# Gates and the first half's u by seven products per 2x2 block, in a hybrid attention and gMLP block on one Trainium2 core

## Chip, cores and metric

The kernel runs on one core of one Trainium2 chip. The metric is device time in microseconds: the median of the runs shown. Everything is float32; matmuls take float32 operands split into a high and a low part in a rounded 32-bit form (fp32r), so that one exact product costs three matmuls: high x high, high x low and low x high.

## The reference, cut to what matters

```python
h = rmsnorm(x, norm_pre_mix)                      # x: 2048 tokens x 1024
proj = h @ w_in                                   # 1024 -> 5376 columns
q, k, v = rope(proj[Q]), rope(proj[K]), proj[V]   # 12 heads of 64, in 3 groups of dilation 1, 4, 16
u, z = gelu(proj[U]), gelu(proj[Z])               # 512 columns each
gate_a, gate_b = sigmoid(proj[GA]), sigmoid(proj[GB])   # 1024 columns each
y_attn = dilated_window_attention(q, k, v)        # three groups, combined by a softmax over log-denominators
y_gmlp = u * (w_spatial @ layernorm(z) + b_spatial)     # per chunk of 128 tokens, causal
merged = gate_a * (y_attn @ w_branch_attn) + gate_b * (y_gmlp @ w_branch_gmlp)
x = x + rmsnorm(merged @ w_out, norm_post_mix)
a = relu(rmsnorm(x, norm_pre_mlp) @ w_mlp_in)
return x + rmsnorm((a * a) @ w_mlp_out, norm_post_mlp)
```

## The kernel before, in words

Tokens are taken in four chunks `c` of 512; chunks 0 and 1 are the first half (`half` 0), 2 and 3 the second (`half` 1). The columns of `w_in` lie in 21 slabs of 256: 0 to 5 are q and k, 6 to 8 v, 9 and 10 u, 11 and 12 z, 13 to 20 the gates. A slab of 256 columns and a half of two chunks make a 2x2 block of outputs (two column groups `m` of 128, two chunks), and the depth of 1024 splits into two parts of four K-tiles of 128.

**Projections (0 to 422 us).** Per half: normalized tokens are transposed into `hT[c]` (high and low, 4 MB a chunk) by `prenorm_cols`; `v_block` makes v, then `qk_pair` makes q and k with the rope, one slab and chunk at a time, while `load_w` brings the next slab and splits it (high on GpSimd, low on VectorE). `keep_cols` writes a raw copy of chunks 0 and 1 to `hT_d` in DRAM, since only two chunks stay on chip.

**The filler.** `filler` is a generator over `queue`: u and z of the second half, the eight gate slabs for the second half, the same eight for the first half, then u and z of the first half. One step is one K-tile: three matmuls (`mm3`). Every slab of a half is 2 x 2 x 8 = 32 steps, 96 matmuls. `reload_h` brings chunks 0 and 1 back from `hT_d` and splits them again on GpSimd, when the first half's turn comes. Each output of 128 x 512 is evicted by ScalarE and written to `gate_d` or `u_d`; the sigmoid is applied later, in the merge.

**Attention (from about 515 us).** 48 units `(g, c, j)`: three groups, four blocks of 512 queries, four heads. TensorE's order is written out by hand: the scores of unit n, one filler step, the transposes `pT` of the exponentials of unit n-1, six filler steps, its product `pv` with v, two filler steps, its transposes back `po`. Keys and queries are loaded two units ahead (`attn_load`). Scores, transposes, `pv` and `po` use four PSUM banks (`aux`), the filler four others (`mm`). The four engines beside TensorE get their order from the scheduler of the framework, with the priorities of the program text; `behind()` ties a group of instructions behind what has been issued.

**Combination (about 990 to 1058 us).** For each chunk `combine` loads the three groups' outputs (`A`, two places), scales and adds them on VectorE (some adds on GpSimd), transposes the sum on TensorE and writes `ya_d`. Between the chunks stand 33, 21, 20 and 24 filler steps. Then z of the first half, the gMLP's `sz_out`, the merge with the gates, `w_out`, and the MLP, which already makes its products by seven instead of eight.

The DMA queue of SyncE (`sp.dma_start`) takes most loads and stores, in order of issue; ScalarE (`act`) and GpSimd (`pool`) can issue too. The page calls it SPq, ACTq and POOLq.

## Time and profile before

| | |
|---|---|
| median of 3 runs | 2687.41 us (2686.49 to 2688.89) |
| the profiled execution | 2693.87 us |
| its span, first to last instruction | 2692.1 us |
| mean granted TensorE clock | 0.998 |
| matmuls of the gates | 514 to 1013 us |
| u of the first half | 1014 to 1060 us |
| z of the first half | 1060 to 1104 us |
| moved by DMA | 431.77 MB, 160 GB/s over the span |

An engine is named PE (TensorE), PEld (its weight loads), DVE (VectorE), ACT (ScalarE), POOL (GpSimd) or SP (SyncE). Busy is the time in which the engine ran an instruction. In a group's row, what stands behind the second bar is the time for which the engine sat idle just ahead of those instructions, and what ended it. The DMA share is the mean busy share of the 16 DMA engines.

### The profile page before, as it was taken

To read this page: it belongs to the slowest core of one execution; us is meant where nothing else is said; L and a number is where in the kernel's file an instruction comes from. 1 tells how busy PE (TensorE), PEld (TensorE's weight loads), DVE (VectorE), ACT (ScalarE), POOL (GpSimd) and SP (SyncE) were. 2 spreads that over 40 slices of the span, in tenths; PEclk is the share of its full clock that TensorE was granted. 3 is DMA by queue.
4 is the path that set the end of the run, shared out by engine and by line. 5 is a ranking of instruction groups with operands and counts; after the bars stand their busy time and mean duration, and the time that the engine had idled before them with its cause. 6 is when DMAs were issued, how large, how long until landed. Compare 5 with 4: busy or idle time off the path is not lost. (4 is left out here: it accounts for less than half of the span.)

```text
span 2692.1 us, 34831 instructions
## 1 busy us (share of the span) xinstructions
PE 2660.2 (99%) x12674; PEld 2222.2 (83%) x12674; DVE 1591.5 (59%) x2677; ACT 1052.7 (39%) x2149; POOL 979.1 (36%) x843
## 2 busy tenths in 40 slices
PE   9999999999999999999999999999999999999998
PEld 7888888888888888888778888888888888888886
DVE  5665463334444435665567765555437888888866
ACT  5212111144444422344445555555545333233334
POOL 0352253200050004310233464323314776676644
PEclk9999999999999999999999999999999999999999
DMA  7445446366587846644576465554343212222235
GB/s 270 169 141 184 152 141 212 99 192 200 172 253 202 219 150 202 211 158 140 189 241 242 141 204 168 181 179 129 108 145 120 87 56 87 93 86 87 87 111 210
DMA packets 299198, 431.77 MB, mean 160 GB/s; under 512 B 52818, under 2 KB 166226, under 8 KB 299027
## 3 DMA queue, kind: packets, MB, share of 16 engines
q1 hardware_dynamic: 226000, 367.34, 43.1%
q10 hardware_dynamic: 64178, 32.06, 4.0%
q0 software_dynamic: 8848, 30.15, 2.9%
q8 instruction: 100, 1.64, 0.3%
q14 instruction: 72, 0.58, 0.1%
HBM read 286.67 MB, written 142.80 MB: 160 GB/s over the span
## 5 line engine op out<-in xcount | busy, mean ns | idle before, releaser
L1637 PE MATMUL ya<-T_spots,s 128*128 128x512 f32 x1176 | 289.2, 389 | 0.7 <-ACT T_spots L70 0.5
L1637 PEld LDWEIGHTS ya<-T_spots,s 128*128 128x128 f32 x1176 | 220.5, 188 | 47.3 <-ACT T_spots L70 0.9
L70 ACT ACTIVATE s<-sraw 128x768 fp32r<-128x768 f32 (+1 forms) x184 | 127.2, 696 | 330.3 <-POOL sraw L1438 156.0
L78 DVE TENSOR_TENSOR s<-sraw,s 128x512 fp32r<-128x512 f32 x172 | 184.3, 1096 | 8.5 <-ACT s L70 8.5
L1112 PE MATMUL aa<-B,A 128*128 128x512 f32 x768 | 182.0, 389 | 0.7 <-DVE A L85 0.7
L1112 PEld LDWEIGHTS aa<-B,A 128*128 128x128 f32 x768 | 143.9, 188 | 30.9 <-DVE A L85 1.1
L1637 PE MATMUL yc<-T_spots,s 128*128 128x512 f32 x624 | 159.6, 389 | 0.0
L72 POOL TENSOR_SCALAR w_g<-w_g_r 128x1024 fp32r<-128x1024 f32 x32 | 34.1, 1081 | 344.8 <-PE g L97 258.1
L1083 POOL TENSOR_TENSOR s<-w1r 128x512 f32<-128x512 f32 x32 | 42.3, 1323 | 308.8 <-DVE S L78 269.2
L95 PE MATMUL x<-hT_a,wq 128*128 128x512 f32 x384 | 149.7, 390 | 0.0
L96 PE MATMUL x<-hT_a,wq 128*128 128x512 f32 x384 | 149.4, 389 | 0.0
L97 PE MATMUL x<-hT_a,wq 128*128 128x512 f32 x384 | 149.4, 389 | 0.0
L709 DVE TENSOR_REDUCE o<-po 128x256 f32<-128x512 f32 x48 | 33.1, 691 | 184.5 <-PE po L708 184.5
L1637 PEld LDWEIGHTS yc<-T_spots,s 128*128 128x128 f32 x624 | 117.1, 188 | 24.3
L70 ACT ACTIVATE hl<-r 128x512 fp32r<-128x512 f32 x48 | 30.4, 633 | 238.1 <-POOL r L307 89.0
L78 POOL TENSOR_TENSOR T_spots<-w2r,T_spots 128x512 fp32r<-128x512 f32 x70 | 104.5, 1520 | 7.3 <-ACT T_spots L70 7.3
L95 PE MATMUL g<-hT_b,w_g 128*128 128x512 f32 x256 | 104.7, 409 | 0.0
L95 PE MATMUL g<-hT_a,w_g 128*128 128x512 f32 x256 | 104.2, 407 | 0.0
L95 PE MATMUL o<-wo,mg 128*128 128x512 f32 x256 | 101.2, 395 | 3.1 <-ACT mg L70 3.1
L70 ACT ACTIVATE S<-w1r 128x512 fp32r<-128x512 f32 x96 | 60.1, 629 | 104.8 <-PE ac L1112 62.9
L97 PE MATMUL o<-wo,mg 128*128 128x512 f32 x256 | 100.7, 394 | 0.0
L1437 POOL TENSOR_TENSOR sraw<-sraw 128x256 f32<-128x256 f32 x56 | 41.8, 746 | 161.7 <-DVE s L78 158.7
(391 smaller groups left out, 7218.9 us busy)
## 6 DMA issues: line engine op xcount, KB each, us to landing
w1r<-in_w_mlp_in_dram SPq DMA_DIRECT2D x64, 512.0 KB, 3.6
sraw<-sd SPq DMA_DIRECT2D x128, 256.0 KB, 3.3
qk<-hl SPq DMA_DIRECT2D x24, 1024.0 KB, 5.1
qq<-qk SPq DMA_DIRECT2D x96, 256.0 KB, 4.9
w_g_r<-in_w_in_dram SPq DMA_DIRECT2D x32, 512.0 KB, 4.9
gated<-gt SPq DMA_DIRECT2D x64, 256.0 KB, 3.4
w2r<-in_w_mlp_out_dram SPq DMA_DIRECT2D x16, 1024.0 KB, 6.3
sd<-u ACTq DMA_DIRECT2D x63, 256.0 KB, 3.5
```

Source lines behind the costliest of these rows:

```text
L70: act.activation(hi, src, AF.Copy)
L72: pool.tensor_scalar(hi, src, 1.0, 1.0, op0=OP.mult, op1=OP.mult)
L78: (pool if lo_eng == "pool" else dve).tensor_sub(lo, src, f32(hi))
L95: pe.matmul(ps, lh, rh, start=start, stop=False)
L96: pe.matmul(ps, lh, rl, start=False, stop=False)
L97: pe.matmul(ps, ll, rh, start=False, stop=stop)
L709: dve.tensor_reduce(ot[:, :, j * 64:(j + 1) * 64], po.rearrange("p (b h e) -> p b e h", b=4, h=2), axis=AX.X, op=OP.add)
L1083: pool.tensor_add(s1, a21, a22)
L1112: pe.matmul(p, w[:, l, k, :], h[:, r, k, :], start=i in (1, 6, 5) and not k and not n, stop=k == 3 and n == 2, skip_group_check=True)
L1437: pool.tensor_add(a22, a21, a22)
L1637: pe.matmul(p, s[:, l], w[r], start=i in (1, 2, 5) and not m and not o, stop=m == 1 and o == 2, skip_group_check=True)
```

## The change

Every 2x2 block of the gates in both halves, and of u in the first half, is made by seven products (Winograd's form of Strassen's) in place of eight. A product is one combination of four weight blocks (128 columns by four K-tiles, a "piece") with one combination of four token blocks (512 tokens by four K-tiles, an "operand"). The seven products are made in four phases, `(1, 2), (6, 7), (5, 3), (4,)`; in a phase one token operand serves all eight pairs of columns (second half) or ten (first half, with u) in turn, and the partial results wait in SBUF (`xs`, `zs`, `vs`), added up by VectorE.

- The sums of token blocks (`pre_t`) and of weight blocks (`pre_s`) are made ahead by VectorE and written to DRAM (`tg_d`, `sg_d`, `s1g_d`) by GpSimd's queue: 28 makers while q and k are projected, 8 more during u of the second half. High and low of chunks 0, 1 and half of 3 go to `hb_d`, raw copies of all four chunks to `hT_d`.
- In the gates each product loads its piece four products ahead, 128 x 512 values in runs of 512 B (2 KB for operand 5), and splits it three products ahead, high and low on GpSimd (high on ScalarE at the two ends). Operands are loaded a phase ahead; those from `tg_d` are split by ScalarE and GpSimd.
- `reload_h` loads high and low ready-made and splits nothing.
- From unit 4 on five filler steps stand between `pT` and `pv` instead of six. The combination gets four places for `A`, all loaded and worked on ahead, with 40, 12, 12 and 11 filler steps. `kp` has three places instead of four.

The diff, cut to its core:

```diff
--- before.py
+++ after.py
...
-    hT_d = dtile([2, P, KT, 512], "hTd")
+    hT_d = dtile([4, P, KT, 512], "hTd")
+    hb_d = dtile([4, P, 2, KT, 512], "hbd")
+    tg_d = dtile([2, P, 4, 4, 512], "tgd")
+    sg_d = dtile([10, P, 2, 4, 256], "sgd")
+    s1g_d = dtile([10, P, 4, P], "s1gd")
...
+        if i == 3:
+            ks = slice(4 if c == 3 else 0, KT)
+            if c != 2:
+                for o in range(2):
+                    sp.dma_start(hb_d[c][:, o, ks], f32(h)[:, o, ks])
...
-            if c < 2:
+            if c == 2 and i % 2:
+                raw = rp.tile([P, 4, P], F32, name=f"hr_{c}{i}{k}", tag="vt", bufs=2)
+            else:
                 raw = xp.tile([P, 4, P], F32, name=f"hr_{c}{i}{k}", tag="hr", bufs=3)
-                act.activation(raw, p3, AF.Copy)
-                sp.dma_start(hT_d[c, :, k:k + 4, i * P:(i + 1) * P], raw)
+            act.activation(raw, p3, AF.Copy)
+            (sp if c < 2 else act).dma_start(hT_d[c, :, k:k + 4, i * P:(i + 1) * P], raw)
...
         for k in range(0, KT, 2):
-            split_in(hT[c][:, :, k:k + 2], hT_d[c, :, k:k + 2, :], None, "pool", "pool")
+            for o in range(2):
+                sp.dma_start(f32(hT[c])[:, o, k:k + 2], hb_d[c][:, o, k:k + 2])
+    def w_at(n):
+        return 13 + n if n < 8 else 1 + n
...
+        def pre_t(half, k, j):
+            w = pre.tile([P, 5 if half else 4, 256], F32, name=f"pt{half}{k}{j}", tag="pre")
+            tsl = slice(j * 256, (j + 1) * 256)
+            for c in range(2):
+                sp.dma_start(w[:, 2 * c:2 * c + 2], hT_d[2 * half + c][:, k::4, tsl])
+            yield
+            b11, b21, b12, b22 = (w[:, n] for n in range(4))
+            dve.tensor_sub(b11, b12, b11)
+            dve.tensor_sub(b12, b22, b12)
+            dve.tensor_sub(b22, b22, b11)
+            dve.tensor_sub(b21, b21, b22)
+            yield
+            pool.dma_start(tg_d[half][:, :, k, tsl], w[:, :4])
+            yield
+        def pre_s(n, k):
+            w = pre.tile([P, 5, 256], F32, name=f"ps{n}{k}", tag="pre")
+            both = w[:, :4].rearrange("p (h k) c -> p h (k c)", h=2)
+            sp.dma_start(both, a["w_in"][w_at(n)].rearrange("p (h k) c -> p h k c", h=2)[:, :, k:k + 2].rearrange("p h k c -> p h (k c)"))
+            yield
+            a11, a21, a12, a22 = (w[:, 2 * kk:2 * kk + 2, m * P:(m + 1) * P] for kk in range(2) for m in range(2))
+            s1 = w[:, 4].rearrange("p (k c) -> p k c", k=2)
+            dve.tensor_add(s1, a21, a22)
+            dve.tensor_sub(a21, a11, a21)
+            dve.tensor_sub(a11, s1, a11)
+            dve.tensor_sub(a12, a12, a11)
+            yield
+            pool.dma_start(sg_d[n][:, :, k:k + 2].rearrange("p h k c -> p h (k c)"), both)
+            pool.dma_start(s1g_d[n][:, k:k + 2], s1)
+            yield
...
+        halves = [[(h_, k, j) for k in range(4) for j in range(2)] for h_ in range(2)]
+        makers = [lambda n=n, k=k: pre_s(n, k) for n in range(10) for k in (0, 2)]
+        makers[12:12] = [lambda z=z: pre_t(*z) for z in halves[1]]
+        flow = []
+        def pre_step():
+            with behind():
+                if makers:
+                    flow.append(makers.pop(0)())
+                for g in reversed(flow):
+                    next(g)
+                if len(flow) == 3 or not makers:
+                    flow.pop(0)
...
                 qk_pair(rp, w, g, which, 2 * half, ropes[2 * half])
+                pre_step()
...
+                pre_step()
+                if half and n % 3 == 2:
+                    pre_step()
+        while flow:
+            pre_step()
+        makers += [lambda z=z: pre_t(*z) for z in halves[0]]
...
-            (dve if c < 2 and g % 2 else pool).tensor_mul(t, t, ut)
+            (dve if c == 3 or c < 2 and g % 2 else pool).tensor_mul(t, t, ut)
...
     queue = [(9, "u", 0, 1), (10, "u", 1, 1), (11, "z", 0, 1), (12, "z", 1, 1)]
-    queue += [(13 + n, "g", n, 1) for n in range(8)] + [(13 + n, "g", n, 0) for n in range(8)]
-    queue += [(9, "u", 0, 0), (10, "u", 1, 0), (11, "z", 0, 0), (12, "z", 1, 0)]
+    queue += [(13, "g", 0, 1)]
+    queue += [(11, "z", 0, 0), (12, "z", 1, 0)]
...
+    PHASES = ((1, 2), (6, 7), (5, 3), (4,))
+    def lagged(ops, pairs):
+        first = [(n, (ops[0], n)) for n in range(pairs)]
+        return [z for _, z in sorted(first + [(n + 1.5, (i, n)) for n in range(pairs) for i in ops[1:]])]
+    PAIRS = {1: 8, 0: 10}
+    PIECES, SPLITS = 4, 3
+    seq = [(half, i, n) for half in (1, 0) for ops in PHASES for i, n in lagged(ops, PAIRS[half])]
+    LAST = len(seq) - PAIRS[0]
+    g_ = dict(raw={}, w={}, b={})
+    def piece(t):
+        if t >= len(seq):
+            return
+        half, i, n = seq[t]
+        raws = g_["raws"]
+        r = raws[t % 4] if t < 8 else raws[4 + (t - LAST - 4) % 5] if t >= LAST + 4 else raws[(t - 8) % 5]
+        if i < 3:
+            src = w_src(w_at(n), i - 1)[:, :, :P]
+        elif i == 5:
+            src = s1g_d[n]
+        else:
+            kk, m = {6: (0, 0), 7: (0, 1), 3: (1, 0), 4: (1, 1)}[i]
+            src = sg_d[n][:, kk, :, m * P:(m + 1) * P]
+        sp.dma_start(r.rearrange("p (k c) -> p k c", k=4), src)
+        g_["raw"][t] = r
+    def split_piece(t):
+        if t >= len(seq):
+            return
+        if t == 4:
+            g_["spots"].append(wp.tile([P, 4, 2, 4, P], F32R, name="spots1", tag="w", bufs=3))
+        at_ = t % 4 if t >= LAST else t % 8
+        w = g_["spots"][at_ // 4][:, at_ % 4]
+        split(w[:, 0], w[:, 1], g_["raw"].pop(t).rearrange("p (k c) -> p k c", k=4),
+              "act" if t < 12 or t > LAST - 10 else "pool", "pool")
+        g_["w"][t] = w
+    def operand(half, i, slot):
+        c = 2 * half
+        g_["b"][half, i] = slot
+        if i in (1, 2, 3):
+            src = hb_d[c + (i == 3)][:, :, (0, 4, 4)[i - 1]:][:, :, :4]
+            for o in range(2):
+                sp.dma_start(f32(slot)[:, o], src[:, o])
+            return []
+        src = tg_d[half][:, (5, 4, 7, 6).index(i)]
+        for k in range(0, 4, 2):
+            sp.dma_start(f32(slot)[:, 1, k:k + 2], src[:, k:k + 2])
+        return [(slot, k) for k in (0, 2)]
...
+    def gates_ahead():
+        g_["spots"] = [wp.tile([P, 4, 2, 4, P], F32R, name="spots0", tag="w", bufs=3)]
+        g_["raws"] = [w[:, m] for w in (wp.tile([P, 2, 512], F32, name=f"gr{n}", tag="raw", bufs=2) for n in range(2))
+                      for m in range(2)]
+        for t in range(PIECES):
+            piece(t)
+        for t in range(SPLITS):
+            split_piece(t)
+    def gates():
+        bank, todo, out_ = {}, [], []
+        slots = [None, hp.tile([P, 2, 2, 4, 512], F32R, name="opB", tag="hT", bufs=2)]
+        zs = wp.tile([P, 8, 512], F32, name="gz", tag="w", bufs=3)
+        zs = [zs[:, n] for n in range(8)]
+        xs = [st.tile([P, 512], F32, name=f"gx{n}", tag="ev", bufs=3) for n in range(3)]
+        g_["b"].update({(1, 1): hT[2][:, :, :4], (1, 2): hT[2][:, :, 4:]})
+        phases = [(half, ops) for half in (1, 0) for ops in PHASES]
+        starts, t = {}, 0
+        for n, (half, ops) in enumerate(phases):
+            starts[t] = n
+            t += PAIRS[half] * len(ops)
+        for t, (half, i, n) in enumerate(seq):
+            if t in starts:
+                ph, t0 = starts[t], t
+                if ph + 1 < len(phases):
+                    s = (ph + 1) % 2
+                    if not slots[s]:
+                        slots[s] = hp.tile([P, 2, 2, 4, 512], F32R, name="opA", tag="hT", bufs=2)
+                    for j, i2 in enumerate(phases[ph + 1][1]):
+                        todo += operand(phases[ph + 1][0], i2, slots[s][:, j])
+                else:
+                    reload_h(0)
+            elif todo and (t - t0) % 3 == 1 and t > t0 + 1:
+                w, k = todo.pop(0)
+                with behind():
+                    split(w[:, 0, k:k + 2], w[:, 1, k:k + 2], f32(w)[:, 1, k:k + 2], "act", "pool")
+            if t == LAST + 2:
+                want(5)
+            piece(t + PIECES)
+            split_piece(t + SPLITS)
+            if i in (1, 6, 5, 4):
+                bank[n] = psum_mm(f"g{half}{i}{n}")
+            p, w, h = bank[n], g_["w"].pop(t), g_["b"][half, i]
+            for k in range(4):
+                for m, (l, r) in enumerate(((0, 0), (0, 1), (1, 0))):
+                    pe.matmul(p, w[:, l, k], h[:, r, k], start=i in (1, 6, 5, 4) and not k and not m,
+                              stop=k == 3 and m == 2, skip_group_check=True)
+                if (t, k) == (3, 2) and late:
+                    sz_out(*late.pop(0))
+                yield
+            if t == 3:
+                a = [ga.tile([P, 512], F32, name=f"ga{n_}", tag=f"ga{n_}", bufs=1) for n_ in range(12)]
+                xs += a[:7]
+                zs += a[7:9]
+                vs = a[9:11]
+                g_["raws"] += a[11:] + vs + zs[8:]
+            x, z, fn = xs[n], zs[n], AF.Copy if n < 8 else AF.Gelu_apprx_tanh
+            while out_:
+                sp.dma_start(*out_.pop())
+            if i == 1:
+                act.activation(x, p, AF.Copy)
+            elif i == 2:
+                act.activation(z, p, fn)
+                o = z, 0, 0
+            elif i == 6:
+                dve.tensor_add(z, x, p)
+            elif i == 7:
+                dve.tensor_add(x, x, p)
+            elif i == 5:
+                v = vs[n % 2]
+                dve.tensor_add(v, x, p)
+                o = v, 1, 1
+            elif i == 3:
+                dve.tensor_add(z, z, p)
+                o = z, 0, 1
+            else:
+                dve.tensor_add(x, x, p)
+                o = x, 1, 0
+            if n > 7 and i in (5, 3, 4):
+                act.activation(o[0], o[0], fn)
+            if i in (2, 5, 3, 4):
+                c, dst = 2 * half + o[2], gate_d if n < 8 else u_d
+                out_.append((dst[n % 8 * 2 + o[1], :, c * 512:(c + 1) * 512], o[0]))
+        sp.dma_start(*out_.pop())
+        yield
...
+            if kind == "g":
+                yield from gates()
+                continue
...
+                if not half:
+                    reload_h(1)
                 for ci in range(2):
-                    yield from z_chunk(zps[half], w, half * 2 + ci)
+                    for k, _ in enumerate(z_chunk(zps[half], w, half * 2 + ci)):
+                        yield
+                        if half and k == 10 and (makers or flow):
+                            pre_step()
+                    if half and not ci:
+                        gates_ahead()
...
+            for c in (2, 3):
                 for m in range(2):
-                    p = psum_mm(f"{kind}_{n}{m}{c}")
-                    for sn, _ in enumerate(steps_T(w, m, c, p)):
-                        if kind == "g" and m == 1 and sn == 6 and late:
-                            sz_out(*late.pop(0))
-                        yield
-                    t = st.tile([P, 512], F32, name=f"{kind}t_{n}{m}{c}", tag="ev", bufs=3)
-                    act.activation(t, p, AF.Copy if kind == "g" else AF.Gelu_apprx_tanh)
-                    dst = gate_d if kind == "g" else u_d
-                    sp.dma_start(dst[n * 2 + m, :, c * 512:(c + 1) * 512], t)
+                    p = psum_mm(f"u_{n}{m}{c}")
+                    yield from steps_T(w, m, c, p)
+                    t = st.tile([P, 512], F32, name=f"ut_{n}{m}{c}", tag="ev", bufs=3)
+                    act.activation(t, p, AF.Gelu_apprx_tanh)
+                    sp.dma_start(u_d[n * 2 + m, :, c * 512:(c + 1) * 512], t)
+                    pre_step()
...
-        kp = at1.tile([P, 5 * P], F32R, name=f"kp_{nm}", tag="akp", bufs=4)
+        kp = at1.tile([P, 5 * P], F32R, name=f"kp_{nm}", tag="akp", bufs=3)
...
-        A = cb.tile([P, 4, 3, 264], F32, name=f"A_{c}", tag="cA", bufs=2)
+        A = cb.tile([P, 4, 3, 264], F32, name=f"A_{c}", tag="cA", bufs=4)
...
-            steps(6 if n > 1 else 9)
+            steps((6 if n < 4 else 5) if n > 1 else 9)
...
     cs = [combine(c) for c in (2, 3, 0, 1)]
     for n in range(2):
+        for z in cs:
+            next(z)
+    for n in range(4):
+        steps((40, 12, 12, 11)[n])
         next(cs[n])
-        next(cs[n])
-    for n in range(4):
-        steps((33, 21, 20, 24)[n])
-        next(cs[n])
-        if n < 2:
-            next(cs[n + 2])
-            next(cs[n + 2])
     ec.close()
+    ega.close()
```

More of the change, by code (lines that the diff above doesn't have):

```diff
@@ L521, in want @@
             else:
[L522 removed]
+                loaded[q] = load_w(wi, f"w_{kind}{n}{half}")
+    PHASES = ((1, 2), (6, 7), (5, 3), (4,))
[5 more added lines that the diff above has]
+    seq = [(half, i, n) for half in (1, 0) for ops in PHASES for i, n in lagged(ops, PAIRS[half])]
```

14 lines of the change are left out of this document (7 added, 7 removed).

## The prediction

> **What bounds the kernel now.** I read the page first, then the busy times by stretch, then the groups of instructions, then one attention unit on the timeline, then the DMA queues.
>
> ```profile
> span 2692.1 us, 34831 instructions
> PE 2660.2 (99%) x12674; PEld 2222.2 (83%) x12674; DVE 1591.5 (59%) x2677; ACT 1052.7 (39%) x2149; POOL 979.1 (36%) x843
> ```
>
> The profiled execution took 2693.87 us, 1.8 us more than this span and 6.46 us more than the median of the runs (2687.41); I sum against 2693.87 and take off 6.46 at the end. TensorE is the bound. The next answer is the busy time by stretch (stretch; its length; busy us and count of PE, PEld, DVE, ACT, POOL; clock; DMA share; GB/s):
>
> ```profile
> 25.00:50.00 25.00, 24.47 (x148) 21.45 (x147) 12.94 (x32) 12.34 (x30) 0.00 (x0) 1.00 0.91 302
> 300.00:400.00 100.00, 100.00 (x443) 82.81 (x442) 57.47 (x65) 11.39 (x18) 47.31 (x28) 1.00 0.45 150
> 400.00:500.00 100.00, 100.00 (x441) 82.44 (x440) 35.34 (x49) 15.84 (x24) 23.61 (x15) 1.00 0.46 155
> 514.00:1014.00 500.00, 498.06 (x2799) 428.01 (x2798) 210.58 (x675) 202.99 (x615) 76.32 (x61) 1.00 0.68 198
> 775.00:800.00 25.00, 25.00 (x149) 21.73 (x148) 12.65 (x35) 10.16 (x31) 22.78 (x14) 1.00 0.89 292
> 800.00:825.00 25.00, 25.00 (x145) 21.68 (x145) 10.49 (x29) 11.70 (x37) 2.08 (x2) 1.00 0.76 203
> 825.00:975.00 150.00, 149.27 (x834) 127.42 (x833) 59.36 (x228) 62.42 (x202) 10.30 (x10) 1.00 0.69 187
> 1014.00:1060.00 46.00, 46.00 (x216) 38.34 (x215) 26.15 (x64) 14.63 (x21) 20.93 (x10) 1.00 0.70 220
> ```
>
> From 514 to 1060 us lie the 48 attention units with the gates as filler, then the combination over the first half's u. TensorE idles 2 us of the first 500; DVE, ACT and POOL are 42%, 41% and 15% busy. So a matmul taken out here shortens the kernel by its own pitch, unless a new wait appears. The pitch is not the 389 ns of a single matmul, since they overlap: 400 to 500 us is unbroken 128x512 matmuls, 441 in 100 us, 0.2268 us each.
>
> **What is removed.** The groups by line and shape (count; busy, mean ns; idle before):
>
> ```profile
> L95 PE MATMUL g<-hT_b,w_g 128*128 128x512 f32 x256 | 104.7, 409 | 0.0
> L549 ACT ACTIVATE gt<-g 128x512 f32<-128x512 f32 x64 | 37.9, 593 | 62.6 <-PE g L97 47.0 <-issue 10.2 <-DMA gated<-gt 4.8
> L78 DVE TENSOR_TENSOR w_g<-w_g_r,w_g 128x1024 fp32r<-128x1024 f32 x30 | 45.1, 1521 | 47.0 <-POOL w_g L72 40.9 <-DMA kp<-qk 6.1
> L72 POOL TENSOR_SCALAR w_g<-w_g_r 128x1024 fp32r<-128x1024 f32 x32 | 34.1, 1081 | 344.8 <-PE g L97 258.1 <-DMA kp<-qk 56.9 <-PE u L97 19.7
> ```
>
> A group of 256 is one of three terms for eight pairs in one half: 96 matmuls per pair and half. The code has 18 such blocks (eight gate pairs in two halves, two u pairs in one): 1728 matmuls. After it, 126 products of 4 K-tiles by 3 terms: 1512. 216 matmuls go, at 0.2268: **-49.0 us**, all inside that stage. That is 72 filler steps: 45 units give one each (45), the combination gets 75 instead of 98 (23), and the rest is u's steps that no longer follow.
>
> **What is added, where PE does not wait.** Nearest rows for the new instructions:
>
> ```profile
> L72 POOL TENSOR_SCALAR yt<-yt x6: 612/620/786, 1085.6 to 1094.1; 128x512 fp32r<-128x512 f32 x6
> L78 POOL TENSOR_TENSOR T_spots<-w2r,T_spots 128x512 fp32r<-128x512 f32 x70 | 104.5, 1520 | 7.3 <-ACT T_spots L70 7.3
> L1642 DVE TENSOR_TENSOR acc_yt<-acc_yt,ya 128x512 f32<-128x512 f32 x72 | 48.4, 685 | 24.2 <-PE ya L1637 24.2
> L737 DVE TENSOR_TENSOR A<-A,E 128x256 f32<-128x256 f32 x48 | 16.8, 426 | 0.0
> L980 POOL DMA_DIRECT2D td<-tq x32 | 17.8, 557 | 1.9 <-POOL tq L975 1.9
> L229 ACT ACTIVATE hr<-pt 128x512 f32<-128x512 f32 x16 | 8.7, 602 | 0.0
> ```
>
> - Weight pieces: 126 splits of 128x512 on POOL, 0.62 + 1.52 = 2.14 us each (some 20 highs go to ACT). A unit hides two products and will last about 8.9 us: POOL 48% busy. From 775 to 800 POOL was busy 22.78 of 25 us and PE never stopped, so this is hidden. A split is asked for three products (13 us) ahead.
> - Sums over products: five of seven end in a DVE add, 90 x 0.685 = 62 us, while DVE loses 30 x 1.52 = 45.6 us of weight splits. Even, in shorter pieces. ACT loses 64 copies and gains 34; u's eight GELUs stay eight.
> - First part: 36 makers of four 128x256 sums, 1.7 us of DVE each and one or two POOL issues of about 0.56 us; 28 of them stand in the projections, hardly more than one for each 10.9 us (48 matmuls). DVE goes from 57% to about 73%, POOL from 47% to about 55%. Behind the DVE sums, which wait for a load issued 10.9 us earlier, queue the rope products that free two of the four banks; they have 10.9 us of room too. On ACT 16 copies more of 0.60 us. Cost 0 to 6 us, I take 1.
>
> **Where it can wait: the attention unit.** One unit of the first group (start; us; engine; line):
>
> ```profile
> 632.74 0.88 PE L702 MATMUL pv<-ph,v 128*128 128x256 f32 x6
> 637.38 1.03 PE L683 MATMUL pT<-ident,e 128*128 128x128 f32 x8
> 642.34 0.88 PE L702 MATMUL pv<-ph,v 128*128 128x256 f32 x6
> 643.06 0.61 PE L702 MATMUL pv<-pf,v 128*128 128x128 f32 x4
> 640.53 0.37 ACT L688 ACTIVATE ph<-pT 128x256 fp32r<-128x256 f32 x1
> 641.40 0.38 ACT L696 ACTIVATE pf<-pT 128x256 f32<-128x256 f32 x1
> 640.94 0.42 DVE L689 TENSOR_TENSOR ph<-pT,ph 128x256 fp32r<-128x256 f32 x1 [1.55 <-ACT ph L688]
> PE pT L683 <- DVE o L709: 1.3, 2, 0.6
> ```
>
> The period is 9.60 us. Between pT and pv stand six filler steps; with five, pv comes 0.68 us sooner, at 641.66. Its inputs are ready at 641.36 (DVE) and 641.78 (ACT, not read until 643.06, then 642.38). So 0.3 and 0.6 us of room stay, and a DVE add can fall into the 1.55 us in which DVE waited. Bounds: nothing, or all of the 0.68 us given back in the 28 units of the first two groups that are shortened, 19 us. Near the first end, by the slack: **+3**. In the third group, copies and no lows, I take nothing. The last line is a wait for a bank; one step still stands there.
>
> **Where it can wait: the queues.** Queues (packets, MB, share) and issues (count, KB, us to landing):
>
> ```profile
> q1 hardware_dynamic: 226000, 367.34, 43.1%
> q10 hardware_dynamic: 64178, 32.06, 4.0%
> w_g_r<-in_w_in_dram SPq DMA_DIRECT2D x32, 512.0 KB, 4.9
> hT_b<-hTd SPq DMA_DIRECT2D x8, 512.0 KB, 6.8
> v<-vd SPq DMA_DIRECT2D x9, 1024.0 KB, 7.2
> ```
>
> By the two stretches 514 to 1060 moved 99 + 10 = 109 MB, 200 GB/s. Pieces are read per half again: 126 x 0.262 = 33.0 MB for 18.9 of weights. Token operands: 6.3 MB in the second half, 10.5 in the first; h of the first half comes back as highs and lows, but only one chunk of it, 4.2 MB, as both raw chunks did. Together +31: 140 MB in 497 us, **282 GB/s**. At 198 GB/s for a share of 0.68 a full share is 291; the row of 775 to 800 shows 292 with PE unbroken. The third group (825 to 975) goes by the same working from 0.69 to about 0.95. So it fits, without much room: an operand burst of 4.2 MB (half change, 14 us at 292) stands ahead of a piece wanted 18 us after its issue, and ahead of keys two units ahead. Price from nothing to 25 us; between, and nearer the first as 292 was carried: **+5**, and **+1** for that burst.
>
> The pieces are runs of 512 B, where weights were read in runs of 1 KB. The second queue's packets average 500 B and took 4.0% of 2692 us for 32.06 MB, 298 GB/s; the first queue's, 1625 B, 317 GB/s: 6% less. The Trainium skill (Perfetto Trace Analysis, DMA Optimizations) says that transfers under 2 KB carry significant overhead each; it speaks against this change, and by it 282 would not be reached. The trace so far doesn't bear it out at 500 B, and I sum by the trace.
>
> **Combination and GELU.**
>
> ```profile
> 987.24 0.60 PE L708 MATMUL po<-ident,pvs 128*128 128x128 f32 x4
> 1002.30 4.11 DVE L737 TENSOR_TENSOR A<-A,E 128x256 f32<-128x256 f32 x12
> 1010.17 1.03 PE L745 MATMUL yt<-ident,A 128*128 128x128 f32 x8
> 1019.45 1.28 ACT L549 ACT_TABLE_LOAD   x1 [4.82 <-PE u L97]
> 1020.74 0.60 ACT L549 ACTIVATE ut<-u 128x512 f32<-128x512 f32 x1
> ```
>
> The first transposes followed the last po by 23 us under 33 steps; 40 steps give 27. The others are then due each 9 us; one chunk costs DVE 4.1 for scaling and about 4.5 for the rest, so with a product's add every 2.7 us it is even, but with four places all loads start at once. Right behind, a 4.2 MB reload must land within the 32 steps (22 us) of the first z chunk. 0 to 10 us, I take **1**. Six of the eight GELUs fall in the combination, two at the third group's start, each with up to two table loads of 1.28 us: 0 to 5, **1**. The Trainium skill (ScalarE: Activation LUTs, What ACT_TABLE_LOAD costs) adds a drain of about 1.38 us to a load; here the next activation starts 1.29 us after the load does, and the sum by the page would be about 1 us more.
>
> **Sum.** -49.0 + 1 + 3 + 5 + 1 + 1 + 1 = -37. 2693.87 - 37 = 2656.9 profiled; less 6.46: **2650 us**.
>
> **Rivals.**
> 1. *The queues bound the stage, still a gain.* At 267 GB/s (from 800 to 825 us a share of 0.76 moved 203) 140 MB take 524 us instead of 497: 27 us back, and 7 for the other terms: 2693.87 - 49 + 34 - 6.46 = 2672. Chance 0.10.
> 2. *The queues bound it and it is slower.* The point is 140 MB in 546 us, 256 GB/s, 12% under what a full share gave. Small runs, half of them writes beside reads, at 240 GB/s: 583 us, 37 more than now, and 7: 2687.4 + 44 = 2731; at 250, 2708. For: 282 asked without pause, which no long stretch shows. Against: 302 and 292 GB/s in 25 us stretches. Chance 0.15. The rule on transfers under 2 KB from the Trainium skill's Perfetto Trace Analysis, above, would end here.
> 3. *The unit's chain sets the period.* 9.6 us stay in the first two groups: 19 us instead of 3: 2666. For: 0.3 us of room. Against: PE's waits in the whole stage are 2 us. Chance 0.07.
>
> The forecast, losses of 0 to 25 us, has 0.68.
>
> **How the numbers follow.** Every cost at zero gives 2638, the low end. Rivals 1 and 3 lie inside; the high end 2690 takes in all the upper bounds together but for rival 2, which is what is left out. A change under 0.2% (5.4 us) is about what cannot be told from none. Faster 0.82 (forecast, rivals 1 and 3, less a little for mixtures), same 0.03, slower 0.15.
>
> **What would show it.** Right: 1512 matmuls in the gates, PE over 97% busy in the stage, which ends 40 us or more sooner, DMA share near 0.9. Wrong: PE waiting for pieces (`spots`) or operands whose DMA landed late (rivals 1, 2), pv waiting for ph or pf with a period of 9.6 (rival 3), PE idle before 514 us (first part), yt waiting for A.

## The result, and the profile after

The changed kernel takes 2679.28 us (median of 9 runs, 2676.15 to 2686.36) beside 2688.01 for the kernel before on the same chip: ratio 0.9970, 95% interval 0.9960 to 0.9981, a gain of 8.7 us where 37 were forecast. The time lies inside the range and the sign is right; three quarters of the gain are missing. The profiled execution took 2676.26 us. The page, and the first and the third queue (packets, MB, share):

```profile
span 2674.5 us, 35483 instructions
PE 2621.4 (98%) x12458; PEld 2188.0 (82%) x12458; DVE 1677.4 (63%) x2881; ACT 1077.5 (40%) x2184; POOL 1196.8 (45%) x1078
q1 hardware_dynamic: 300048, 431.84, 49.2%
q10 hardware_dynamic: 72626, 36.25, 4.5%
```

216 matmuls fewer, as counted (12674 to 12458), and PE's busy time falls by 38.8 us, but the span is only partly filled. The busy time by stretch, columns as before, shows where it is not:

```profile
450.00:475.00 25.00, 21.70 (x96) 17.64 (x94) 5.67 (x10) 3.92 (x7) 5.35 (x7) 0.99 1.02 357
475.00:500.00 25.00, 23.11 (x90) 18.31 (x91) 10.23 (x25) 4.72 (x7) 9.88 (x14) 0.87 0.90 294
500.00:525.00 25.00, 22.65 (x108) 19.21 (x107) 14.22 (x40) 4.45 (x8) 4.67 (x5) 0.93 0.79 271
725.00:750.00 25.00, 25.00 (x150) 21.82 (x148) 12.73 (x39) 10.80 (x36) 5.77 (x6) 1.00 0.98 327
750.00:775.00 25.00, 25.00 (x150) 21.82 (x149) 10.99 (x36) 12.48 (x39) 16.98 (x18) 1.00 1.01 315
975.00:1000.00 25.00, 16.18 (x72) 13.07 (x70) 20.13 (x68) 7.74 (x11) 7.40 (x3) 0.87 0.99 330
1000.00:1025.00 25.00, 19.94 (x88) 16.24 (x88) 23.88 (x45) 7.24 (x11) 16.30 (x9) 0.86 0.81 282
1025.00:1050.00 25.00, 20.07 (x80) 15.55 (x81) 13.26 (x19) 5.84 (x11) 8.19 (x6) 0.86 0.65 221
```

Attention, which was to be the hard place, holds: PE is busy 25.00 of 25 us at DMA shares of 0.98 and 1.01, at 327 and 315 GB/s; its longest wait in that stage is 3.3 us, at 944 us. PE stops in u and z of the second half (450 to 525 us) and in the combination (975 to 1050), and in both the granted clock falls, at the lowest to 0.86 or 0.87. From PE's timeline, the marks of the stages in us:

| | first gate product | last `pv` of attention | first matmul of z, first half |
|---|---|---|---|
| before | 514.15 | 984.97 | 1060.00 |
| after | 526.23 | 967.86 | 1049.08 |

So up to the gates +12.1; attention 470.8 to 441.6, -29.2; combination 75.0 to 81.2, +6.2: together -10.9. With z of the first half, 44.6 to 46.9 us, it is -8.6, about what the medians show. The two profiled executions differ by 17.6: the other 9.0 lie behind z, in code that the change does not touch, and the executions themselves lie 5.9 above and 3.0 us below their medians.

What PE waited for, in the two places (total, times, longest):

```profile
PE rowsum L538 <- POOL wsp L533: 5.2, 1, 5.2
PE sz L552 <- DVE z L580: 2.4, 1, 2.4
PE g L698 <- DVE ga L723: 12.7, 1, 12.7
PE g L698 <- DVE gx L729: 4.6, 1, 4.6
```

None of these waits has a term in the prediction.

### The profile page after: what moved, and what is told of

The parts are those of the page before. It is cut to its first block, busy times and chain, and to the rows that moved or that the text cites. A ratio compares the mean times of both kernels' runs of the same rounds, so it can differ in the third digit from the quotient of the medians.

```text
span 2674.5 us, 35483 instructions
## 1 busy us (share of the span) xinstructions
PE 2621.4 (98%) x12458; PEld 2188.0 (82%) x12458; DVE 1677.4 (63%) x2881; ACT 1077.5 (40%) x2184; POOL 1196.8 (45%) x1078
## 3 DMA queue, kind: packets, MB, share of 16 engines
q10 hardware_dynamic: 72626, 36.25, 4.5%
## 5 line engine op out<-in xcount | busy, mean ns | idle before, releaser
L698 PE MATMUL g<-opA,spots 128*128 128x512 f32 x672 | 171.8, 400 | 12.7 <-DVE ga L723 12.7
L698 PE MATMUL g<-opB,spots 128*128 128x512 f32 x648 | 168.3, 403 | 6.1 <-DVE gx L729 4.6
L698 PEld LDWEIGHTS g<-opA,spots 128*128 128x128 f32 x672 | 122.2, 190 | 35.1 <-issue 13.1
L78 POOL TENSOR_TENSOR spots<-gr,spots 128x512 fp32r<-128x512 f32 x98 | 130.3, 1335 | 41.3 <-ACT spots L70 26.7
L698 PEld LDWEIGHTS g<-opB,spots 128*128 128x128 f32 x648 | 118.6, 192 | 29.5 <-issue 5.0
L72 POOL TENSOR_SCALAR wq<-wq_r 128x1024 fp32r<-128x1024 f32 x24 | 31.5, 1317 | 184.1 <-PE va L97 133.4
```

The costliest lines, as they stand in the source:

```text
L72: pool.tensor_scalar(hi, src, 1.0, 1.0, op0=OP.mult, op1=OP.mult)
L78: (pool if lo_eng == "pool" else dve).tensor_sub(lo, src, f32(hi))
L698: pe.matmul(p, w[:, l, k], h[:, r, k], start=i in (1, 6, 5, 4) and not k and not m, stop=k == 3 and m == 2, skip_group_check=True)
```

## The experiments

Eighteen kernels, each timed beside the kernel before. Ratios are to that kernel, with 95% intervals; the changed kernel has 0.9970. Each expectation names a theory (T) and its rival (R), with what each would give.

### u and z of the second half

The row sums need the spatial weights `wsp`, and z's product `sz` needs z normalised by DVE. Who held them up, from the waits of SP's queue (440 to 480 us) and of DVE (455 to 515 us):

```profile
SPq L451 <- DMA sgd<-ps: 8.4, 2, 6.3
DVE pt L439 <- DMA pt<-hTd: 27.8, 5, 12.3
```

Here SP issues in order: a maker's load (L451, L436) waits until its place is free, that is until an older maker's store has landed, and the load of `wsp`, behind it, went out at 468.0 us and landed 7.7 us later. DVE takes its work in order too: for 27.8 us it stood at the sums of the eight makers of the first half, waiting for their loads, and z's statistics stood behind.

**Row sums later (e4).** `next(sg)` moved from step 72 to step 112.

> The row sums of z's second half are taken 40 product steps later, with everything else in place. T2a (the 5.2 us wait for the row-sum weights and the low clock after it are the cost in the u and z stage): about 8 us faster than the changed kernel, 2671 us. R2a (the next wait, for the normalised z, comes as late as before, since DVE waits in order for the token operand's loads): under 3 us, 2676 us or more.

Measured 2680.07 us, ratio 0.9970 (0.9960 to 0.9981). R2a: the wait for `wsp` is gone and the wait of `sz` for z grew from 2.4 to 10.1 us.

**All makers in the projections (e3).**

```diff
+        makers[:0] = [lambda z=z: pre_t(*z) for z in halves[0]]
...
                 pre_step()
+                pre_step()      # one more per n
```

> All 36 makers of the token operand run inside the projections, none is left for the stage that computes u and z of the second half. T2 (the makers' loads and their DVE sums that lie in that stage cost it 12 us): idle time of PE between 450 and 525 us falls from 8 to under 2 us, the clock there stays above 0.95, 10 to 12 us faster than the changed kernel, 2667 to 2669 us. R2 (the queue is full at 452 to 468 us for other loads and the wait for the row-sum weights stays): 0 to 4 us, 2675 us or more.

Measured 2703.94 us, 1.0057 (1.0044 to 1.0070): 25 us slower than the changed kernel. In its own stage T2 holds: from the first matmul of z of the second half to the first gate product pass 48.0 us as in the kernel before, in place of 60.1, with no wait. But z starts at 504.2 instead of 466.1 us, since PE now stops in the projections. Its waits between 140 and 280 us:

```profile
PE x L95 <- DVE t L318: 8.3, 2, 5.0
PE pt L218 <- ACT hr L240: 7.7, 1, 7.7
PE va L95 <- DVE vt L358: 1.9, 1, 1.9
```

28 makers hide in the projections and 36 do not: the rope's products (`t`) then stand on DVE behind sums that wait for their loads (19.2 us of such waits between 140 and 280 us), the very queue that the prediction named and priced at 0 to 6 us.

**No makers for the first half (e6), later products (e8), and both (e10).** e8 puts the row sums at step 112 and the product of chunk 2's z behind the last z block:

```diff
-            if i == 2 and late and c > 1:
+            if i == (3 if c == 3 else 2) and late and c > 1:
```

> Leaves out the eight makers of the first half's token sums, which run while u and z of the second half are made; the first half's operands read the second half's sums in their place, so that the products and the loads in the gates stay the same. T2b (these makers' loads and sums make the whole loss of the u and z stage): that stage shortens by 10 to 12 us, no wait over 1 us in 450 to 525 us, 2667 to 2669 us. R2b (the loads are late for other traffic and the row-sum wait stays): 0 to 4 us, 2675 us or more.

> PE's order alone is changed: the row sums of the second half 40 steps later, and the product of chunk 2's normalised z with the spatial weights 8 steps later, behind the last z block. T2c (PE's two waits are for things that come a fixed time late, behind the token operand's loads on SP and DVE, so that products put in front fill the wait): 450 to 525 us without idle time over 2 us, 6 to 10 us faster than the changed kernel, 2669 to 2673 us. R2c (as with the row sums alone, the wait only moves to the next): 2676 us or more.

> Leaves out the eight makers of the first half's token sums (the first half reads the second half's sums in their place), and puts the row sums 40 steps and the product of chunk 2's normalised z 8 steps later. T2d (the loss in u and z of the second half is these makers twice over: SP's queue held up by loads that wait for a place, which brings the spatial weights late, and DVE's queue held up by their sums): no wait is left in 450 to 525 us, and the time is the changed kernel's less 11 to 13 us, 2666 to 2668 us. R2d (other loads make part of it): 2671 us or more.

e6: 2675.10 us, 0.9948 (0.9936 to 0.9960), at the edge of R2b, 4.2 us under the changed kernel, since the wait for `wsp` stayed at 6.0 us: the last makers of the weights, too, hold SP (its waits at L451 are 8.7 us). e8: 2674.70 us, 0.9947 (0.9934 to 0.9959), 4.6 us under it and between T2c and R2c; `sz` still waits 4.4 us. e10: 2666.46 us, 0.9915 (0.9902 to 0.9929), 12.8 us under the changed kernel, as T2d had it. Its stretches from 450 to 525 us:

```profile
450.00:475.00 25.00, 25.00 (x112) 20.71 (x111) 7.37 (x14) 2.47 (x5) 6.71 (x9) 1.00 0.99 331
475.00:500.00 25.00, 25.00 (x112) 20.72 (x111) 7.18 (x20) 8.46 (x13) 6.05 (x8) 1.00 0.73 239
500.00:525.00 25.00, 25.00 (x127) 20.92 (x126) 10.72 (x23) 7.81 (x13) 10.07 (x9) 1.00 0.38 126
```

No idle time at all. From the first matmul of z to the first gate product pass 47.9 us, beside 48.0 in the kernel before, 60.1 in the changed kernel, 56.0 in e6 and 55.0 in e8. With e3 that settles this place: 12 us, from makers that hold up two in-order queues. A single remedy gains little more than a third, because behind the first wait stands the second.

### The combination

In the kernel before the filler's outputs were evicted by ScalarE, so no bank of the filler was freed by DVE; DVE could wait for the combination's loads while PE stayed busy, 75.00 of 75 us (`A`, before, 985 to 1060 us):

```profile
DVE M L720 <- DMA A<-att: 13.7, 2, 10.7
```

Now every second product of a pair writes the bank from which DVE must first read the first one (`ga`, L723), and that read stands in DVE's order among the work on four chunks. PE stops at 991.2 us; DVE, without a pause, ends one chunk's adds, does the statistics of two more and the scaling of one, and comes to the add that PE waits for at 1003.03 (rows of DVE's timeline, with others left out between them):

```profile
990.93 1.78 DVE L960 TENSOR_TENSOR A<-A 128x1024 f32<-128x1024 f32 x1
996.77 4.11 DVE L957 TENSOR_TENSOR A<-A,E 128x256 f32<-128x256 f32 x12
1000.96 2.15 DVE L940 TENSOR_TENSOR M<-A 128x16 f32<-128x16 f32 x1
1003.03 0.68 DVE L723 TENSOR_TENSOR ga<-ga,g 128x512 f32<-128x512 f32 x1
```

**Interleaving (e1) and adds off GpSimd (e2).** e1 loads four chunks, then takes them one at a time with 16, 16, 14, 14 and 15 steps between; e2 has `eng = dve` for all chunks.

> The combination of one query group's four chunks is interleaved with the first half's product steps: all four loads ahead, chunk 2's arithmetic, 16 steps, chunk 3's, 16 steps, and so on; the number of steps is the same 75. T1 (DVE works in order, and the adds that end a product group stand behind all four chunks' arithmetic): idle time of PE between 970 and 1050 us falls from 17 us to under 4 us, the granted clock of that stretch rises from 0.86 to above 0.95, and the time falls by 15 to 24 us against the changed kernel, to 2655 to 2665 us. R1 (it is GpSimd's long adds that stretch DVE's small operations, wherever they stand): idle time stays above 8 us and the gain is under 8 us, 2671 us or more.

> All adds of the combination go to DVE, none to GpSimd; the order stays. R1 (GpSimd's adds of 128x1024 stretch DVE's 128x16 operations from 0.17 to about 2.4 us): the stretched operations vanish, PE's idle time in 970 to 1050 us falls under 8 us, 2662 to 2670 us. T1 (the queue on DVE): the four adds moved to DVE lengthen its queue by about as much as the stretched operations shorten it; 2679 to 2685 us, idle 15 us or more.

e1: 2676.06 us, 0.9956 (0.9944 to 0.9968); PE still waits 10.2 us for `ga`. e2: 2676.55 us, 0.9951 (0.9938 to 0.9964); the wait is 19.1 us. e1 ends in R1's range; e2 ends in neither's, though the wait is as T1 said: both theories fall in their simple form. e1 did not free the add that PE waits for: the first chunk's loads let DVE begin at 982.37 us, and two chunks' scaling still stands in front of that add, at 1002.91. DVE's small operations in the combination, before, after and in e2, and the adds of the last two (count; busy, mean ns; idle before):

```profile
L724 DVE TENSOR_TENSOR E<-A,M 128x16 f32<-128x16 f32 x12 | 1.4, 172 | 0.1
L733 DVE TENSOR_TENSOR E<-E,M 128x16 f32<-128x16 f32 x12 | 1.4, 170 | 0.1
L721 DVE TENSOR_TENSOR M<-M,A 128x16 f32<-128x16 f32 x4 | 0.7, 174 | 2.6 <-DMA A<-att 2.6
```

```profile
L941 DVE TENSOR_TENSOR M<-M,A 128x16 f32<-128x16 f32 x4 | 4.0, 990 | 0.4 <-DMA A<-att 0.4
L953 DVE TENSOR_TENSOR E<-E,M 128x16 f32<-128x16 f32 x12 | 4.0, 382 | 0.0
L944 DVE TENSOR_TENSOR E<-A,M 128x16 f32<-128x16 f32 x12 | 3.6, 353 | 0.1
L960 DVE TENSOR_TENSOR A<-A 128x1024 f32<-128x1024 f32 x2 | 3.2, 1616 | 0.0
L959 DVE TENSOR_TENSOR A<-A 128x1024 f32<-128x1024 f32 x2 | 2.4, 1212 | 0.0
```

```profile
L953 DVE TENSOR_TENSOR E<-E,M 128x16 f32<-128x16 f32 x12 | 3.0, 305 | 0.0
L941 DVE TENSOR_TENSOR M<-M,A 128x16 f32<-128x16 f32 x4 | 1.7, 433 | 0.4 <-DMA A<-att 0.4
L944 DVE TENSOR_TENSOR E<-A,M 128x16 f32<-128x16 f32 x12 | 1.4, 169 | 0.1
L960 DVE TENSOR_TENSOR A<-A 128x1024 f32<-128x1024 f32 x4 | 5.9, 1469 | 0.0
L959 DVE TENSOR_TENSOR A<-A 128x1024 f32<-128x1024 f32 x4 | 4.9, 1216 | 0.0
```

The three groups cost 3.5 us before, 11.6 after, 6.1 in e2. e2 gives 5.5 us back there and pays 5.2 for the two chunks' adds (10.8 in place of 5.6): even.

**Fewer chunks ahead of z (e5, f4; with e8's order in f3 and f4).** e5 and f3 combine chunks 0 and 1 during z, in halves of 256 tokens; f4 only chunk 1.

> Only chunks 2 and 3 are combined ahead of z of the first half; chunks 0 and 1 are combined in halves of 256 tokens during z, where DVE is busy 9 of 25 us. T3 (the combination stage is bound by the amount of work on DVE, not by its order nor by GpSimd: 58 of 75 us busy against 42 of 85 in the kernel before): PE's idle time between 970 and 1050 us falls from 18 us to under 6 us, z of the first half grows by under 4 us, and the time falls by 10 to 20 us against the changed kernel, to 2659 to 2669 us. R3 (the first wait is for the loads that come 15 us late, and the same work on DVE only moves on): idle stays over 10 us, 2673 us or more.

> Two chunks combined during z, and the later row sums and spatial products, together. If T2c and T3 hold, their gains lie in separate stages and add up: 2650 to 2663 us. If either falls, the time is that of the other alone.

> Three chunks are combined ahead of z of the first half, the fourth in two halves during z with all its adds on DVE; row sums and chunk 2's spatial product later as in the run before. T3c (the amount of DVE work bounds the combination; the loss of the last trial was the wait for loads and GpSimd's adds inside z): idle time in 970 to 1050 us falls from 18 us to under 10 us, z of the first half has no wait over 2 us, 2662 to 2669 us. R3c: z pays what the combination gains, 2673 us or more.

e5: 2699.58 us, 1.0041 (1.0025 to 1.0056). f3: 2697.51, 1.0030 (1.0019 to 1.0042). f4: 2682.74, 0.9986 (0.9975 to 0.9997). In the combination T3 holds in part: in e5 the wait for `ga` falls to 2.3 us, and from the last `pv` to z pass 70.3 us in place of 81.2 (2 us of that are two chunks' transposes that have left); but PE waits 5.6 us for a weight piece (`spots`) instead, and 9.5 us stay idle, not under 6. And z pays more than the combination gains, 77.1 us for 46.9: its transposes wait for GpSimd's adds, which stand behind the weight splits.

```profile
PE yt L965 <- POOL A L960: 19.7, 2, 16.8
```

f4 ends as R3c had it: combination 70.9 us, z 54.0, and 14 us more behind z than in the changed kernel, which no run follows up.

**More steps (e11), spread out (f5, f6).** From unit 24 on (in f6 from unit 4) four filler steps stand before `pv` instead of five, and the combination gets 100 (120) steps. e11 keeps the order (49, 18, 18, 15); f5 and f6 have e8's order and, in the program text, take one chunk's arithmetic every 18 (f6: 22) steps.

> 25 product steps are moved out of attention (four in place of five between the units' transposes and their product with v, from unit 24 on) into the combination, which has 100 in place of 75. T3b (DVE's work per product step bounds the combination, and the units' chain has room): PE's idle time between the last unit and z of the first half falls from 18 us to under 8 us while attention's stretches stay at 25.00 of 25 busy, 2665 to 2672 us. R3b (the units' chain takes 8.3 us or more by itself): attention loses what the combination gains, 2677 us or more.

> The later row sums and spatial product; 25 product steps moved out of attention as before; and the combination's four chunks spread over its 100 steps: all loads first, 26 steps, one chunk's arithmetic, 18 steps, the next one's, and so on. T4 (a chunk's arithmetic is about 9 us of DVE in one piece, and all products' adds stand behind it; with 18 steps, 12.4 us, for each chunk DVE keeps up, and with 16 steps or with four chunks in a row it does not): idle time between the last unit and z of the first half under 8 us, attention still 16 us shorter, 2655 to 2664 us. R4 (GpSimd's long adds stretch DVE's work so that spreading does not help): idle 15 us or more, 2672 us or more.

> The same with 45 steps moved (from unit 4 on) and 22 steps for each chunk. T4: idle time between the last unit and z under 5 us; attention 30 us shorter if the units' chain still has room at four steps in the first groups too, 2652 to 2662 us. R4b (in the first two groups the chain or the loads take the room): attention is shortened by less than 22 us, and the time is above that of the run with 25 steps.

e11: 2687.01 us, 0.9996 (0.9987 to 1.0006). f5: 2681.95, 0.9974 (0.9965 to 0.9984). f6: 2690.32, 1.0001 (0.9991 to 1.0011). In e11 attention takes 425.2 us instead of 441.6: 16.4 less for 25 steps of 0.68, so the units' chain had room for them. In f6 it takes 421.8, 19.8 less for 45 steps: in the first groups it has no room for a second step (R4b). All was lost again in the combination: 107.9, 106.1 and 118.9 us, where the moved steps account for 17, 17 and 31. PE waits for the same add; f5, and two rows of its DVE timeline:

```profile
PE g L698 <- DVE ga L723: 18.7, 3, 11.6
980.16 4.11 DVE L957 TENSOR_TENSOR A<-A,E 128x256 f32<-128x256 f32 x12
986.42 0.67 DVE L723 TENSOR_TENSOR ga<-ga,g 128x512 f32<-128x512 f32 x1
```

T4's numbers are missed, but f5 does not test T4. PE's long stop comes about 35 steps behind the last unit, where the text has one chunk's arithmetic in front (the second stands at step 44). In the trace DVE has by then done the second chunk's statistics and scaling and begun on the other two, and only then the add: the scheduler, which gives DVE its order, took the chunks together again. What was left to explain: in e11, f5 and f6, as in the changed kernel, PE's longest wait in the combination is for DVE at a product, never at a chunk's own transposes.

**A longer lag (e12, f7, f8).** The second product of a pair follows 2.5 instead of 1.5 products behind the first, 6.8 instead of 4.1 us; alone, with e1 and e8, and with f5.

```diff
-        [(n + 1.5, (i, n)) for n in range(pairs) for i in ops[1:]]
+        [(n + 2.5, (i, n)) for n in range(pairs) for i in ops[1:]]
```

> The changed kernel with the second product of a pair 2.5 in place of 1.5 products behind the first. T5 (both products of a pair use one PSUM bank, so the second must wait until DVE has read the first's; with 1.5 products, 4.1 us, of slack every piece of DVE work longer than that stops PE, and the combination's pieces are 9 us): PE's idle time between the last unit and z falls from 18 us to 8 to 12 us, 2668 to 2675 us. R5 (all four banks are taken anyway, so the lag changes nothing): 2677 to 2682 us.

> The later row sums and spatial product, the interleaved combination (16, 16, 14, 14 and 15 steps), and the lag of 2.5. T5: the waits of DVE's 9 us pieces come one at a time, and 6.8 us of slack covers most of each: idle time under 8 us between the last unit and z, 2658 to 2666 us. R5: as the interleaving and the later products alone would add up, 2670 to 2674 us.

> The run with 25 steps moved and the chunks spread over 100 steps, with the lag of 2.5. T5: the wait for DVE (18.7 us there, all at the adds that the pair's second product needs) falls under 8 us, 2662 to 2671 us. R5: 2679 to 2684 us.

e12: 2685.60 us, 0.9989 (0.9979 to 0.9998), 6 us slower than the changed kernel and above R5's range, with a wait of 13.6 us. f7: 2676.52, 0.9956 (0.9944 to 0.9968), 2.5 us above R5's range. T5 falls in both. f8: 2671.71, 0.9939 (0.9927 to 0.9951), 10 us under f5, where T5 put it but for 0.7 us, though the waits for DVE fell less than it said, from 18.7 to 12.9 us (the two shown and two of 1.3 and 0.3); the best of all the kernels here that compute the whole reference:

```profile
PE g L698 <- DVE gx L729: 5.7, 1, 5.7
PE g L698 <- DVE ga L723: 5.6, 1, 5.6
```

So the coupling through the bank is worth 10 us with f5's steps (combination 106.1 to 96.1 us) and nothing without them (e12). That DVE needs steps in which to catch up is my reading; no run varies that alone.

**Without the scaling (e13), and two places (e14).**

> The changed kernel without the combination's twelve multiplications of 128x256 and two adds of 128x1024 per chunk (the transposes take the first group's output as it is); loads, weights, transposes and stores stay. T6 (this arithmetic on DVE, about 7 of 9 us per chunk, in front of the products' adds, is the combination's whole loss of 24 us): PE's idle time between the last unit and z falls from 18 us to under 4 us, 2655 to 2661 us. R6 (the 15 us that the twelve loads hold SP's queue, and the weight splits, make a good part of it): idle stays over 8 us, 2665 us or more.

> The combination as in the kernel before: two places, two chunks ahead, the next chunk loaded and scaled behind each chunk's transposes, with 25, 16, 15 and 19 steps (the same 75). T7 (with two chunks less in front, DVE reaches the products' adds sooner, but a chunk's load of 15 us and 9 us on DVE do not fit into 31 steps): the first wait falls from 12.7 to under 4 us, and waits of 10 us or more come at the transposes of the third and fourth chunk; 2677 to 2684 us, so that the four places are worth nothing by themselves. R7 (the four places made the loss): 2660 to 2670 us.

e13: 2671.48 us, 0.9933 (0.9921 to 0.9946): 7.8 us under the changed kernel, a third of the loss, and in R6's range. PE still waits in the combination:

```profile
PE g L698 <- DVE E L953: 7.7, 1, 7.7
PE g L698 <- ACT spots L70: 3.8, 1, 3.8
```

Without its heavy work DVE still goes through the chunks' statistics one after another, with waits for loads and for the exponential of ScalarE (2.0 us of waits in the last 7), and the add that PE needs stands nearly at the end (`ga` at 1000.34 us). SP takes 15 us to issue the loads; in the changed kernel, where the first chunk's statistics begin at 979.92 us:

```profile
973.29 15.21 SPq L937 DMA_DIRECT2D A<-att  x12
```

e14: 2686.87 us, 0.9996 (0.9987 to 1.0005), 3 us above T7's range: with two places and these steps the first wait for `ga` is gone and the waits come at the transposes (4.7 and 4.0 us) and for weight pieces (6.5 us). The four places do not make the loss; beside these two they are worth about 7 us by the medians.

## Why the prediction was wrong in size

**The matmuls removed, -49: right.** 1512 in the gates, 216 fewer in the count, all inside the stage.

**The attention unit, +3, and the queues, +5 and +1: right, and too dear.** Of the 30.6 us that 45 steps are worth, 29.2 came. From the first gate product to z, DMA moved 263 GB/s in 523 us at a share of 0.85, 138 MB where 140 were forecast, and up to 327 GB/s in 25 us. Rivals 1 and 2 are refuted by PE's 25.00 of 25 beside a full DMA share and 437 of 442 us over attention, rival 3 by the stage's 29.2; e11 adds that later units had room for yet another step. The rule on transfers under 2 KB, from the Trainium skill's Perfetto Trace Analysis, DMA Optimizations, would have given a slower kernel; the queue of 500 B packets here moved 36.25 MB in 4.5% of 2674.5 us, 301 GB/s, beside 328 for the first queue. So the trace does not agree at that size, if a packet is what the page calls a transfer; a whole piece is 256 KB.

**The first part, +1 with bounds 0 to 6: the step that failed first.** For the projections themselves it was right: z of the second half starts at 466.1 us in both kernels. But the term priced the 28 makers there and left the eight in u and z at nothing, with no cover named, and it followed neither SP's queue past their loads nor DVE's past their sums, though both are in order and both hold something PE needs next. Measured: 12.1 us, shown by e10 and e3. The sign that the prediction gave for it, idle time before 514 us, is what showed it.

**The combination with the reload, +1: the step that failed most.** Its 27 steps fewer (72 less attention's 45) are worth 18.4 us, and instead it grew by 6.2: 24.6 us lost. "Even" compared amounts: DVE's 8.6 us per chunk and an add every 2.7 against 9 us between chunks. The amounts were roughly right, but for the small operations that took 11.6 us for 3.5. What was left out is order and dependence: the products' adds had become something PE waits for within 4.1 us, in the same queue as pieces of 9 us, and behind loads that SP issues for 15 us. Of the 24.6 us, 18.8 are idle time in PE's waits (12.7, 4.6 and two small ones of 0.9 and 0.6), and about 5 are the low clock behind them, next section. By e13 the arithmetic makes 8 (combination 81.2 to 73.3 us). That the rest is the order of what is left is read from DVE's timeline and not shown by a run: no run here freed the add of the work in front of it. Nor is it shown that GpSimd's adds are no part of it: e2 shows that moving them to DVE gains 3 us, and the operation right ahead of `ga` took 2.15 us beside one of them.

**GELU, +1: not seen.** The stage has five table loads in both kernels.

**The range.** Its high end was to take in all upper bounds together; 6, 19, 25, 10 and 5 us on 2638 make 2703, not 2690. The result does not hang on it.

## What to carry to other kernels

When a change hands an engine work that the bottleneck engine waits for, amounts no longer decide: list what stands in front of it in that engine's order, how long each piece is, and how many instructions of slack the buffers give. Follow every new load and store through its issuing queue as well, and past the engine that waits for it. And before counting what the removal of a wait brings, look for the one that stands behind it: in u and z the two single remedies gained 4.2 and 4.6 us of 12, and both together all of it. When an experiment moves work in the program text, look in the trace whether it moved in the engine's order too: in f5 it did not.

## What the hardware showed that was not expected

**A stop costs more than its length.** PE's timeline after, around the two long waits of the combination:

```profile
970.48 20.70 PE L698 MATMUL g<-opA,spots 128*128 128x512 f32 x90
1003.85 4.53 PE L698 MATMUL g<-opA,spots 128*128 128x512 f32 x12 [12.67 <-DVE ga L723]
1013.10 8.43 PE L698 MATMUL g<-opB,spots 128*128 128x512 f32 x36
1028.39 9.95 PE L698 MATMUL g<-opB,spots 128*128 128x512 f32 x30 [4.60 <-DVE gx L729]
```

Unbroken, 90 matmuls take 20.70 us, 0.23 each; behind the stops 12 take 4.53 (0.38) and 30 take 9.95 (0.33), 1.8 and 3.1 us more. The granted clock shows it as 0.86 to 0.87 in the stretches with these stops. Shorter stops, the first row before the change, the others after:

```profile
505.13 3.73 PE L480 MATMUL sz<-wsp,z 128*128 128x128 f32 x32
515.23 5.70 PE L552 MATMUL sz<-wsp,z 128*128 128x128 f32 x32 [2.35 <-DVE z L580]
947.26 0.66 PE L928 MATMUL po<-ident,pvs 128*128 128x128 f32 x4 [3.25 <-ACT pvs L924]
```

`sz` takes 3.73 us where nothing stops ahead of it (before, e3, e10) and 5.70 behind a stop of 2.35 us, at a granted clock of 0.50 from 516 to 519 us; in e5 it takes 6.06 behind 1.43 us. Behind the stop of 3.25 us ahead of `po` the clock stays at 1.00 (944 to 954 us). The Trainium skill (TensorE: Matmul & The Clock Gate, HAM oscillation — how this bites in real kernels) says that gaps of more than about 3.4 us lower the clock for what follows; the trace agrees for the stops of 4.6 us and more, but not that shorter ones are free. What decides which of the short ones cost is not shown.

**GpSimd's long adds and DVE's short operations.** After, the groups of 128x16 rise to means of 353 to 990 ns from 170 to 174 before, and the longest rows, 2.1 to 2.6 us for one to three operations, lie beside GpSimd's adds of 128x1024. In the kernel before none of them runs beside a GpSimd operation. The Trainium skill (GPSIMD Engine Reference, 8. Key points) says that GpSimd shares its SBUF interfaces with VectorE and contends with VectorE's instructions of two SBUF inputs; these are of that kind, and in e2 without the adds L944's mean is back at 169 ns. What stays long there, four rows of 1.0 to 2.0 us at L940, L941 and L953, lies beside GpSimd's weight splits (997.33 us, for one, beside a split from 994.55 to 998.58).
